# Hymba-style encoder: A's key doublings and C's gate product on VectorE, own-key products summed in PSUM, new spacing of A's levels

## The chip, the cores and the metric

The kernel runs on one core of one Trainium2 chip. Its engines are TensorE (PE; its weight loads are shown as PEld), VectorE (DVE), ScalarE (ACT), GpSimd (POOL) and SyncE (SP, which issues most transfers). The metric is the device time of one execution in microseconds: less is better.

## The reference, cut to what matters

Two layers (`DEPTH = 2`) of a mixer over 512 tokens of width 1024. In each layer the normalised input is projected by `w_in` into the inputs of four groups of 512 channels; their outputs are gated, concatenated, projected by `w_out` and added to x.

- A: a gated linear recurrence in both directions, four heads of 128 channels. Per head, with keys `k` and forget gates `f` per channel, `S_t = diag(f_t) S_{t-1} + k_t v_t^T`, `o_t = S_t^T q_t`; the sum of both directions is normalised and gated.
- B: attention within a window of 128 tokens. D: attention to 256 memory tokens.
- C: an mLSTM in both directions, four heads: values `h`, then `(h - mu) * rsqrt(var + eps) * g`, and then the product with the gate `silu(z)`.

The change touches A's recurrence and the last product of C.

## The kernel before, in words

TensorE does almost all work in fp32. A projection is three matmuls for each pair of blocks (high and low parts of weights and activations). The weights come through `load_w`: a transfer into a raw tile `wr` (three buffers), a cast on ScalarE to `wh`, and the remainder `wl = wr - wh` on VectorE, 1024 elements for each partition.

The mixers are generators ("jobs") whose steps are woven into the projections' matmuls by a planner, `Weave`. Each projection calls `tick` after every six small or three large matmuls (640 ns of planned time). A step returns `(pe, lat)`: its own TensorE time, which is added to the planner's clock, and the time after which its next step is due. A due step is emitted at the next tick; `join` emits what is left of a job at once. So `A_LAT` (4300 ns) sets how many projection matmuls stand between two levels of a head in the order in which the program is written. The framework then places each engine's instructions; within an engine they can stand in another order than they were written in, as far as their inputs allow.

`mix_A` works on one head; a pair of heads runs at a time (`group_A`, `pr` 0 and 1), the second one set off by half of `A_LAT`. The products of queries and keys are made by doubling: `K2` (keys, two directions of 512) and `Q2` (queries) hold products of gates over blocks of m tokens. At the start `ks`, the sum of both halves of K2, is made on VectorE, and `per_block` makes the products within single tokens ("own-key products") from it: 16 blocks of 32 x 32 into a PSUM bank of `psc`, which has two. Then for m = 1, 2, 4, ... 64 a level does the following:

- `per_block` with `kc`, an interleaved copy of K2 that ScalarE makes, and Q2 (from m = 32 on with K2 itself);
- the key doubling `k2v` in place, on GpSimd, by gate products `Tm`;
- the query doubling `q2v` in place, on VectorE;
- `copy_predicated` of the level's products into `ac` on VectorE (or a copy into `at`);
- the gate products of the next level, `Tn`, on VectorE (they use the tile of `ks` again as `tot`).

After the levels come transposes of K2, the states, the output products `o`, the normalisation to y, and after `A_LATN` the transposes of y. For the second pair a `join` stands between the projection `group_Dz` and C's next projections; it emits what is left of the pair.

In `stats` of group C a head is normalised on VectorE and multiplied by its gate on GpSimd; its transposes (`finish`) come one head later.

All vector instructions are recorded at line 142 and most matmuls at lines 248 (`mm`) and 251 (`gmm`), so they are told apart by tiles: `s` is a bank of `psc`, `pj` a bank of a projection, `u` and `a` are tiles of 4 KB and 2 KB for each partition (K2, Q2, F2 are `u`; `ks`, q, `ac`, the products are `a`). A key or query doubling is `u<-u,u` at level 1 and `u<-u,a` later; an own-key product is `s<-a,a`.

Of the kernel before, what the change touches and what calls it, by code (L numbers as in the profile page):

```python
# [10 lines left out]
ALU = mybir.AluOpType  # L11
# [3 lines left out]
P = 128  # L15
# [54 lines left out]
              + [O_CK, O_CQ, O_CZ, O_CZ + 256, O_DQ, O_DQ + 256])  # L70
OUT_ORDER = ((0, 1), (2, 3))

A_LAT0, A_LAT, A_LAT2, A_LATN = 5500, 4300, 500, 27000
B_LATP, B_LAT = 300, 1150
AHEAD = 2
AHEAD_V = 1
# [120 lines left out]
def trunk(tc, a, dbg=None, mark=lambda s: None):  # L197
# [6 lines left out]
    with es:  # L204
# [343 lines left out]
        def mix_A(l, hd, F2, K2, q, v, gz, yT):  # L548

            Q2 = u4([2, 512])  # L550
            ks = a2([512])
            dve.tensor_tensor(ks, K2[:, 0], K2[:, 1], ALU.add)
            dve.tensor_tensor(Q2, F2, V(q, 0, [[0, 2], [1, 512]]), ALU.mult)
            scr = u4([2, 512])
            at = scr[:, 1]
            ac = a2([NC, 32])

            kcs = (scr[:, 0], F2[:, 1])
            at4 = at.rearrange("p (c q) -> p c q", c=NC)

            def interleaved(lv, m):
                kc = kcs[lv % 2]
                act.copy(V(kc, 0, [[2 * m, 256 // m], [m, 2], [1, m]]), V(K2, 0, [[2 * m, 256 // m], [512 + m, 2], [1, m]]))
                return kc

            def per_block(n, k, qv):

                p = psc()[:, :NC * n].rearrange("p (c q) -> p c q", c=NC)
                for c in range(NC):
                    for i in range(P // n):  # L570
                        gmm(p[i * n:(i + 1) * n, c], k(c * P + i * n), qv(c * P + i * n), True, True)
                return p
            kc = interleaved(0, 1)
            yield 0, A_LAT0
            pd = per_block(32, lambda b: ks[:, b:b + 32], lambda b: q[:, b:b + 32])
            act.copy(ac, pd)
            Tm = F2
            n = 512
            tot = ks
            toff = 0  # L580
            lv = 0
            m = 1
            while m <= 64:
                k2v = V(K2, 0, [[2 * m, 256 // m], [512 + m, 2], [1, m]])
                q2v = V(Q2, 0, [[2 * m, 256 // m], [512 + m, 2], [1, m]])
                if m <= 16:
                    pl = per_block(32, lambda b: kc[:, b:b + 32],
                                   lambda b: V(Q2, b, [[2 * m, 16 // m], [512 + m, 2], [1, m]]))
                else:

                    d = lambda b: b // m % 2
                    pl = per_block(m, lambda b: K2[:, d(b), b:b + m],
                                   lambda b: Q2[:, 1 - d(b), b + m - 2 * m * d(b):b + 2 * m - 2 * m * d(b)])

                gp.tensor_tensor(k2v, k2v, V(Tm, n + 1, [[2, n // 2], [-(n + 1), 2], [0, m]]), ALU.mult)
                if 1 < m < 16:
                    kc = interleaved(lv + 1, 2 * m)
                dve.tensor_tensor(q2v, q2v, V(Tm, 1, [[2, n // 2], [n - 1, 2], [0, m]]), ALU.mult)
                if m <= 16:
                    dve.copy_predicated(ac, V(cu, lv * 32, [[0, NC], [1, 32]]), pl)  # L600
                    if m == 16:

                        act.copy(at.rearrange("p (c j q) -> p c j q", c=NC, j=4), V(ac, 0, [[32, NC], [0, 4], [1, 32]]))
                elif m == 32:
                    dve.copy_predicated(at.rearrange("p (c j q) -> p c j q", c=NC, j=4),
                                        V(cu, 5 * 32, [[0, NC], [32, 4], [1, 32]]), V(pl, 0, [[32, NC], [0, 4], [1, 32]]))
                else:
                    act.copy(at4[0:64, :, 64:128], pl[0:64])
                    act.copy(at4[64:128, :, 0:64], pl[64:128])

                if m == 1:
                    Tn = q
                else:
                    Tn = tot[:, toff:toff + n]
                    toff += n
                dve.tensor_tensor(Tn[:, 0:n].rearrange("p (d k) -> p d k", d=2),
                                  V(Tm, 0, [[n, 2], [2, n // 2]]), V(Tm, 1, [[n, 2], [2, n // 2]]), ALU.mult)
                if m == 1:
                    kc = interleaved(lv + 1, 2 * m)
                Tm = Tn  # L620
                n //= 2
                m *= 2
                lv += 1
                yield 560, A_LAT


            kb = ((0, 1, 2), (3, 2, 1))
            ktm = F2
            for d in range(2):
                pt = ptr()  # L630
                for i, j in enumerate(kb[d]):
                    nc.tensor.transpose(pt[:, i * P:(i + 1) * P], K2[:, d, j * P:(j + 1) * P], ident)
                act.copy(ktm[:, d, 0:384], pt[:, 0:384])
            yield 640, A_LAT2
            st = K2
            for d in range(2):
                pS = psc()
                for i, j in enumerate(kb[d]):
                    mm(pS[:, i * P:(i + 1) * P], ktm[:, d, i * P:(i + 1) * P], v(j))
                act.copy(st[:, d, 0:P], pS[:, 0:P])  # L640
                for i in range(1, 3):
                    dve.scalar_tensor_tensor(st[:, d, i * P:(i + 1) * P], st[:, d, (i - 1) * P:i * P],
                                             Tm[:, 4 * (1 - d) + kb[d][i]:4 * (1 - d) + kb[d][i] + 1], pS[:, i * P:(i + 1) * P],
                                             ALU.mult, ALU.add)
            yield 1280, A_LAT2
            o = po()
            for c in range(NC):
                oc = o[:, c * P:(c + 1) * P]
                mm(oc, at[:, c * P:(c + 1) * P], v(c), start=True, stop=False)
                qc = [Q2[:, i, c * P:(c + 1) * P] for i in range(2)]  # L650
                if c > 0:
                    mm(oc, qc[1], st[:, 0, (c - 1) * P:c * P], start=False, stop=(c == NC - 1))
                if c < NC - 1:
                    mm(oc, qc[0], st[:, 1, (2 - c) * P:(3 - c) * P], start=False, stop=True)
            ss = sm([4], "ssA")
            jk = scr[:, 0]
            for c in range(NC):
                act.activation(jk[:, c * P:(c + 1) * P], o[:, c * P:(c + 1) * P], AF.Square, accum_out=ss[:, c:c + 1])
            r = rsqrt(4, ss, 1.0 / P, EPS)
            y = F2[:, 0]  # L660
            for c in range(NC):
                dve.scalar_tensor_tensor(y[:, c * P:(c + 1) * P], o[:, c * P:(c + 1) * P], r[:, c:c + 1], gz(c), ALU.mult, ALU.mult)
            yield 2133, A_LATN
            pt = ptr()
            for c in range(NC):
                nc.tensor.transpose(pt[:, c * P:(c + 1) * P], y[:, c * P:(c + 1) * P], ident)
            if len(yT[0]) <= hd // 2:
                for i in range(2):
                    yT[i].append(u4([2, 512], F32R))
            y_evac(yT, hd, 0, T, pt, gA[:, l, hd:hd + 1])  # L670
            yield 427, 0

        def group_A(l, h, pr, yT, between=None, before=None, raw=None):
# [49 lines left out]
            def go():  # L723
                for b in range(2):
                    jobs.append(wv.spawn(f"mixA{pr * 2 + b}", mix_A(l, pr * 2 + b, F2[b], K2[b], q[b],
                                         lambda c, b=b: v[:, c, b * P:(b + 1) * P],
                                         lambda c, b=b: gz[:, c, b * P:(b + 1) * P], yT), after=b * A_LAT / 2))
            if pr == 0:
                gates()
                if raw is not None:  # L730
# [167 lines left out]
        def group_C(l, h):  # L898
# [195 lines left out]
            gz = []  # L1094

            def mixer(yT):
# [47 lines left out]
                def stats(hd):  # L1144

                    hc = H[hd]
                    h3 = hc.rearrange("p (c d) -> p c d", c=NC)
                    s = slice(hd % 2 * P, hd % 2 * P + P)
                    dve.scalar_tensor_tensor(h3, tho[hd // 2][:, :, s], 1.0, h3, ALU.add, ALU.mult)
                    mv = sm([4, 2], "mvC")  # L1150
                    for c in range(NC):
                        b6 = sm([6], "stC")
                        dve.bn_stats(b6, h3[:, c])
                        dve.bn_aggr(mv[:, c], b6)
                    r = rsqrt(4, mv[:, :, 1], 1.0, 4 * EPS)
                    for c in range(NC):
                        dve.tensor_scalar(h3[:, c], h3[:, c], mv[:, c, 0:1], r[:, c:c + 1], ALU.subtract, ALU.mult)
                    gp.tensor_tensor(h3, h3, gz[hd // 2][:, :, s], ALU.mult)

                def finish(hd):  # L1160
                    pt = ptr()
# [410 lines left out]
```

## Time and profile before

| | us |
|---|---|
| median of 3 runs (1136.57 to 1139.35) | 1136.97 |
| profiled execution, its own time | 1137.1 |
| its span, first to last instruction | 1135.3 |
| busy: TensorE | 1079.4 |
| busy: VectorE | 795.3 |
| busy: ScalarE | 538.3 |
| busy: GpSimd | 243.4 |

Times within the trace are from the start of the span. The records of matmuls overlap, so their busy time isn't work at full rate; what counts is where TensorE stands idle and who releases it. The mean granted clock of TensorE is 0.99.

### The profile page before, as it was taken

To read this page: it belongs to the slowest core of one execution; us is meant where nothing else is said; L and a number is where in the kernel's file an instruction comes from. 1 tells how busy PE (TensorE), PEld (TensorE's weight loads), DVE (VectorE), ACT (ScalarE), POOL (GpSimd) and SP (SyncE) were. 2 spreads that over 40 slices of the span, in tenths; PEclk is the share of its full clock that TensorE was granted. 3 is DMA by queue.
4 is the path that set the end of the run, shared out by engine and by line. 5 is a ranking of instruction groups with operands and counts; after the bars stand their busy time and mean duration, and the time that the engine had idled before them with its cause. 6 is when DMAs were issued, how large, how long until landed. Compare 5 with 4: busy or idle time off the path is not lost.

```text
span 1135.3 us, 22387 instructions
## 1 busy us (share of the span) xinstructions
PE 1079.4 (95%) x8886; PEld 968.2 (85%) x8886; DVE 795.3 (70%) x1759; ACT 538.3 (47%) x1138; POOL 243.4 (21%) x276
## 2 busy tenths in 40 slices
PE   6889999989999999999999999999899999999997
PEld 4778988989888888788788889889888788989997
DVE  7799536787486768777464786377968759688664
ACT  5545335666443534344564433376654353442443
POOL 4252000231142123111020241012304311230200
PEclk9999999999999999999999999999999999999998
DMA  7222134111221444422434221311121233362211
GB/s 255 77 94 76 57 104 158 59 57 45 88 75 58 108 107 122 148 76 92 134 128 142 81 67 58 98 62 56 58 75 57 76 108 98 103 195 77 74 38 74
DMA packets 34783, 105.41 MB, mean 93 GB/s; under 512 B 4360, under 2 KB 7816, under 8 KB 34680
## 3 DMA queue, kind: packets, MB, share of 16 engines
q1 hardware_dynamic: 33960, 101.57, 28.4%
q0 software_dynamic: 720, 2.42, 0.6%
q8 instruction: 70, 1.15, 0.4%
q14 instruction: 33, 0.27, 0.1%
HBM read 99.72 MB, written 4.26 MB: 92 GB/s over the span
## 4 chain that ended last, share of the span: by engine, by line
PE 71%; DVE 18%; ACT 3%; issue 2%; DMA 1%; POOL 0%; SPq 0%; DVEq 0%; ACTq 0%; POOLq 0%
PE pj L248 33%; PE pj L251 23%; DVE a L142 7%; DVE u L142 5%; PE o L248 4%; DVE wl L142 3%; PE s L248 3%; PE s L251 2%; ACT wh L142 1%; PE tr L857 1%; PE o L251 1%; ACT u L142 1%; ACT a L142 1%; DVE rq_t L142 1%; PE tr L1290 1%
## 5 line engine op out<-in xcount | busy, mean ns | idle before, releaser
L251 PE MATMUL pj<-wh,u 128*128 128x256 f32 x1984 | 390.7, 287 | 3.2 <-ACT u L142 1.2
L248 PE MATMUL pj<-u,wh 128*128 128x512 f32 (+1 forms) x1216 | 376.8, 391 | 1.0 <-ACT a L142 0.8
L251 PEld LDWEIGHTS pj<-wh,u 128*128 128x128 f32 x1984 | 317.0, 190 | 8.2 <-ACT u L142 2.4
L142 DVE TENSOR_TENSOR wl<-wr,wh 128x1024 fp32r<-128x1024 f32 (+1 forms) x162 | 215.4, 1330 | 135.8 <-ACT wh L142 135.3
L251 PE MATMUL pj<-wl,u 128*128 128x256 f32 x992 | 280.7, 283 | 0.0
L248 PEld LDWEIGHTS pj<-u,wh 128*128 128x128 f32 x1216 | 219.2, 190 | 42.5 <-ACT a L142 1.2
L248 PE MATMUL pj<-u,wl 128*128 128x512 f32 (+1 forms) x608 | 234.0, 385 | 1.8 <-DVE wl L142 1.8
L142 ACT CAST wh<-wr 128x1024 fp32r<-128x1024 f32 (+1 forms) x162 | 164.1, 1014 | 151.1 <-PE pj L248 88.0
L251 PEld LDWEIGHTS pj<-wl,u 128*128 128x128 f32 x992 | 188.3, 190 | 0.8 <-issue 0.3
L248 PEld LDWEIGHTS pj<-u,wl 128*128 128x128 f32 x608 | 115.4, 190 | 25.3 <-DVE wl L142 2.0
L142 POOL TENSOR_TENSOR u<-u,a 128x512 f32<-128x512 f32 (+1 forms) x64 | 93.2, 1464 | 133.0 <-PE s L251 53.5
L142 POOL TENSOR_SCALAR u<-u,rB 128x256 f32<-128x256 f32 (+1 forms) x64 | 37.3, 595 | 232.9 <-DVE rB L142 132.5
L142 POOL TENSOR_TENSOR u<-u,u 128x512 f32<-128x512 f32 x16 | 29.3, 1830 | 210.9 <-DVE a L142 125.0
L248 PE MATMUL pj<-wh,u 128*128 128x256 f32 (+1 forms) x320 | 62.8, 287 | 0.0
L142 DVE TENSOR_TENSOR u<-u,a 128x512 f32<-128x512 f32 (+1 forms) x56 | 50.2, 897 | 15.9 <-PE s L251 13.5
L248 PE MATMUL o<-u,u 128*128 128x129 f32 (+1 forms) x384 | 50.2, 275 | 1.9 <-DVE dnC L142 1.9
L248 PEld LDWEIGHTS o<-u,u 128*128 128x128 f32 x384 | 48.2, 191 | 4.4 <-issue 2.4
L248 PEld LDWEIGHTS pj<-wh,u 128*128 128x128 f32 x320 | 51.0, 188 | 0.7 <-issue 0.5
L251 PEld LDWEIGHTS s<-u,u 128*32 128x32 f32 (+1 forms) x1760 | 27.4, 115 | 28.1 <-issue 19.3
L251 PE MATMUL s<-u,u 128*32 128x32 f32 (+2 forms) x1760 | 35.0, 207 | 17.2 <-DVE a L142 13.6
L142 ACT COPY u<-u 128x512 f32<-128x512 f32 x40 | 27.0, 684 | 40.7 <-DVE u L142 22.8
L248 PE MATMUL pj<-wl,u 128*128 128x256 f32 (+1 forms) x160 | 45.3, 283 | 0.0
(213 smaller groups left out, 1494.3 us busy)
## 6 DMA issues: line engine op xcount, KB each, us to landing
wr<-in_wpk SPq DMA_DIRECT2D x154, 512.0 KB, 3.3
u<-in_xT SPq DMA_DIRECT2D x16, 256.0 KB, 4.6
u<-rdr SPq DMA_DIRECT2D x16, 256.0 KB, 4.5
u<-gdr SPq DMA_DIRECT2D x16, 192.0 KB, 5.8
u<-in_memT SPq DMA_DIRECT2D x4, 512.0 KB
xd<-u POOLq DMA_DIRECT2D x4, 512.0 KB, 4.8
u<-xd SPq DMA_DIRECT2D x4, 512.0 KB, 5.4
out<-u SPq DMA_DIRECT2D x8, 256.0 KB, 2.0
```

The costliest lines, as they stand in the source:

```text
L142: r = f(*args, **kw)
L248: nc.tensor.matmul(out, l, r, start=start, stop=stop)
L251: nc.tensor.matmul(out, l, r, start=start, stop=stop, skip_group_check=True)
L857: nc.tensor.transpose(pt[:, j * P:(j + 1) * P], pr[e][:, j * P:(j + 1) * P], ident)
L1290: nc.tensor.transpose(pt[:, (2 * t + i) * P:(2 * t + i + 1) * P], pr[:, i, t * P:(t + 1) * P], ident)
```

## The change

The key doubling of all seven levels is made by VectorE instead of GpSimd, and so is C's product with the gate. The sum `ks` is gone; `per_block` takes several keys and sums their products in PSUM, so that the own-key products are two matmuls for each block, with the two halves of K2. `tot` gets a tile of its own, allocated after them. `A_LAT` becomes 5400 for the first pair and 4600 for the second, and the offset of a pair's second head becomes half of that.

```diff
--- before.py
+++ after.py
@@ -70,7 +70,7 @@
               + [O_CK, O_CQ, O_CZ, O_CZ + 256, O_DQ, O_DQ + 256])
 OUT_ORDER = ((0, 1), (2, 3))
 
-A_LAT0, A_LAT, A_LAT2, A_LATN = 5500, 4300, 500, 27000
+A_LAT0, A_LAT, A_LAT2, A_LATN = 5500, (5400, 4600), 500, 27000
 B_LATP, B_LAT = 300, 1150
 AHEAD = 2
 AHEAD_V = 1
@@ -548,8 +548,6 @@
         def mix_A(l, hd, F2, K2, q, v, gz, yT):
 
             Q2 = u4([2, 512])
-            ks = a2([512])
-            dve.tensor_tensor(ks, K2[:, 0], K2[:, 1], ALU.add)
             dve.tensor_tensor(Q2, F2, V(q, 0, [[0, 2], [1, 512]]), ALU.mult)
             scr = u4([2, 512])
             at = scr[:, 1]
@@ -563,20 +561,23 @@
                 act.copy(V(kc, 0, [[2 * m, 256 // m], [m, 2], [1, m]]), V(K2, 0, [[2 * m, 256 // m], [512 + m, 2], [1, m]]))
                 return kc
 
-            def per_block(n, k, qv):
+            def per_block(n, qv, *ks):
+
 
                 p = psc()[:, :NC * n].rearrange("p (c q) -> p c q", c=NC)
                 for c in range(NC):
                     for i in range(P // n):
-                        gmm(p[i * n:(i + 1) * n, c], k(c * P + i * n), qv(c * P + i * n), True, True)
+                        for k in ks:
+                            gmm(p[i * n:(i + 1) * n, c], k(c * P + i * n), qv(c * P + i * n), k is ks[0], k is ks[-1])
                 return p
             kc = interleaved(0, 1)
             yield 0, A_LAT0
-            pd = per_block(32, lambda b: ks[:, b:b + 32], lambda b: q[:, b:b + 32])
+
+            pd = per_block(32, lambda b: q[:, b:b + 32], lambda b: K2[:, 0, b:b + 32], lambda b: K2[:, 1, b:b + 32])
             act.copy(ac, pd)
             Tm = F2
             n = 512
-            tot = ks
+            tot = a2([512])
             toff = 0
             lv = 0
             m = 1
@@ -584,15 +585,15 @@
                 k2v = V(K2, 0, [[2 * m, 256 // m], [512 + m, 2], [1, m]])
                 q2v = V(Q2, 0, [[2 * m, 256 // m], [512 + m, 2], [1, m]])
                 if m <= 16:
-                    pl = per_block(32, lambda b: kc[:, b:b + 32],
-                                   lambda b: V(Q2, b, [[2 * m, 16 // m], [512 + m, 2], [1, m]]))
+                    pl = per_block(32, lambda b: V(Q2, b, [[2 * m, 16 // m], [512 + m, 2], [1, m]]),
+                                   lambda b: kc[:, b:b + 32])
                 else:
 
                     d = lambda b: b // m % 2
-                    pl = per_block(m, lambda b: K2[:, d(b), b:b + m],
-                                   lambda b: Q2[:, 1 - d(b), b + m - 2 * m * d(b):b + 2 * m - 2 * m * d(b)])
-
-                gp.tensor_tensor(k2v, k2v, V(Tm, n + 1, [[2, n // 2], [-(n + 1), 2], [0, m]]), ALU.mult)
+                    pl = per_block(m, lambda b: Q2[:, 1 - d(b), b + m - 2 * m * d(b):b + 2 * m - 2 * m * d(b)],
+                                   lambda b: K2[:, d(b), b:b + m])
+
+                dve.tensor_tensor(k2v, k2v, V(Tm, n + 1, [[2, n // 2], [-(n + 1), 2], [0, m]]), ALU.mult)
                 if 1 < m < 16:
                     kc = interleaved(lv + 1, 2 * m)
                 dve.tensor_tensor(q2v, q2v, V(Tm, 1, [[2, n // 2], [n - 1, 2], [0, m]]), ALU.mult)
@@ -621,7 +622,7 @@
                 n //= 2
                 m *= 2
                 lv += 1
-                yield 560, A_LAT
+                yield 560, A_LAT[hd // 2]
 
 
             kb = ((0, 1, 2), (3, 2, 1))
@@ -724,7 +725,7 @@
                 for b in range(2):
                     jobs.append(wv.spawn(f"mixA{pr * 2 + b}", mix_A(l, pr * 2 + b, F2[b], K2[b], q[b],
                                          lambda c, b=b: v[:, c, b * P:(b + 1) * P],
-                                         lambda c, b=b: gz[:, c, b * P:(b + 1) * P], yT), after=b * A_LAT / 2))
+                                         lambda c, b=b: gz[:, c, b * P:(b + 1) * P], yT), after=b * A_LAT[pr] / 2))
             if pr == 0:
                 gates()
                 if raw is not None:
@@ -1155,7 +1156,7 @@
                     r = rsqrt(4, mv[:, :, 1], 1.0, 4 * EPS)
                     for c in range(NC):
                         dve.tensor_scalar(h3[:, c], h3[:, c], mv[:, c, 0:1], r[:, c:c + 1], ALU.subtract, ALU.mult)
-                    gp.tensor_tensor(h3, h3, gz[hd // 2][:, :, s], ALU.mult)
+                    dve.tensor_tensor(h3, h3, gz[hd // 2][:, :, s], ALU.mult)
 
                 def finish(hd):
                     pt = ptr()
```

## Rows read from the trace of the kernel before

**Rows 1.** The page's part 1: busy us, share of the span, instructions.
```profile
PE 1079.4 (95%) x8886; PEld 968.2 (85%) x8886; DVE 795.3 (70%) x1759; ACT 538.3 (47%) x1138; POOL 243.4 (21%) x276
```

**Rows 2.** Busy time by stretch, A's first five levels, instructions in brackets, granted clock.
```profile
60.00:92.00 32.00, 25.36 (x482) 23.30 (x482) 31.14 (x45) 12.93 (x20) 15.34 (x10) 1.00 0.30 98
300.00:332.00 32.00, 29.90 (x480) 27.45 (x479) 27.48 (x36) 14.81 (x23) 17.81 (x10) 1.00 0.21 67
636.00:664.00 28.00, 24.28 (x419) 22.67 (x418) 27.11 (x35) 12.87 (x20) 16.24 (x10) 1.00 0.18 59
856.00:886.00 30.00, 27.40 (x462) 25.80 (x461) 29.18 (x36) 13.50 (x21) 16.91 (x10) 0.94 0.17 58
```
The columns: stretch and its length, then PE, PEld, DVE, ACT, POOL, PE clock, DMA share, GB/s.

**Rows 3.** TensorE's timeline, last pair: start, length, idle before in square brackets, releaser.
```profile
866.50 0.46 PE L251 MATMUL s<-a,a 128*32 128x32 f32 x32
868.76 0.54 PE L251 MATMUL s<-u,u 128*32 128x32 f32 x32 [1.79 <-DVE a L142]
```

**Rows 4.** VectorE's timeline in the same pair.
```profile
863.95 2.91 DVE L142 TENSOR_TENSOR wl<-wr,wh 128x1024 fp32r<-128x1024 f32 x1 [0.34 <-ACT wh L142]
...
868.32 0.29 DVE L142 COPY_PREDICATED a<-cu,s 128x128 f32<-128x128 uint8 x1
...
877.34 0.69 DVE L142 TENSOR_TENSOR u<-u,a 128x512 f32<-128x512 f32 x1
...
883.95 2.12 DVE L142 TENSOR_TENSOR wl<-wr,wh 128x1024 fp32r<-128x1024 f32 x1
```

**Rows 5.** GpSimd's timeline in the same pair.
```profile
863.79 2.00 POOL L142 TENSOR_TENSOR u<-u,u 128x512 f32<-128x512 f32 x1 [3.83 <-DVE a L142]
...
883.35 1.63 POOL L142 TENSOR_TENSOR u<-u,a 128x512 f32<-128x512 f32 x1 [0.68 <-ACT u L142]
```

**Rows 6.** VectorE's groups, 856 to 886: count, busy us, mean ns of one.
```profile
L142 DVE TENSOR_TENSOR wl<-wr,wh 128x1024 fp32r<-128x1024 f32 x4 | 10.0, 2503 | 0.7 <-ACT wh L142 0.7
L142 DVE TENSOR_TENSOR u<-u,a 128x512 f32<-128x512 f32 x4 | 4.4, 1100 | 0.0
L142 DVE TENSOR_TENSOR a<-u 128x512 f32<-128x512 f32 x4 | 4.1, 1018 | 0.0
...
L142 DVE TENSOR_TENSOR u<-u,u 128x512 f32<-128x512 f32 x2 | 2.2, 1090 | 0.0
```

**Rows 7.** All weight splits: nanoseconds, shortest, median, longest.
```profile
L142 DVE TENSOR_TENSOR wl<-wr,wh x162: 410/1225/2985, 7.1 to 1111.4; 128x1024 fp32r<-128x1024 f32 x154, 128x256 fp32r<-128x256 f32 x8
```

**Rows 8.** The chain that ended last, first pair, levels and end: start, length, what.
```profile
95.36 0.39 PE s L251 x32
95.74 3.02 PE pj L251 x24
...
118.43 0.22 PE o L248 x2
118.65 0.71 PE pj L251 x6
119.36 2.05 PE o L248 x18
```

**Rows 9.** TensorE's timeline, first pair, own-key products and level 1.
```profile
63.23 0.46 PE L251 MATMUL s<-a,a 128*32 128x32 f32 x32
63.50 0.56 PE L251 MATMUL s<-u,u 128*32 128x32 f32 x32
```

**Rows 10.** The chain that ended last, end of the last pair.
```profile
916.97 2.01 PE o L248 x18
918.98 5.35 PE pj L248 x23
924.33 0.87 PE tr L666 x8
```

**Rows 11.** VectorE's timeline, end of the last pair and `stats` in C.
```profile
923.06 1.12 DVE L142 SCALAR_TENSOR_TENSOR u<-o,rq_y,u 128x128 f32<-128x128 f32 x4
...
1009.97 1.11 DVE L142 TENSOR_SCALAR u<-u,mvC,rq_y 128x128 f32<-128x128 f32 x4
1011.00 0.16 DVE L142 RECIPROCAL dnC<-dnC 128x2 f32<-128x2 f32 x1
```

## The prediction

> **What bounds the kernel now.** I read the page's engine totals first [rows 1]: TensorE's records cover 95% of the span, VectorE's 70%. The kernel is bound by TensorE, so an edit is worth what it gives TensorE back: idle time before a matmul, added matmuls, or time at the low clock. The totals don't say where that idle lies, so next I cut out the four stretches in which group A runs its first five levels (two heads at once, two pairs, two layers) [rows 2]. TensorE is idle there for 6.64, 2.10, 3.72 and 2.60 us, 15.1 us together. VectorE is nearly full in three of them (31.14 of 32, 27.11 of 28, 29.18 of 30 us). The last stretch also has a mean granted clock of 0.94: in 30 us that is 1.8 us of full-speed clock lost.
>
> What does TensorE wait for? In the last stretch it stands 1.79 us before the level-1 products of the second head, and the releaser is a VectorE write of an `a` tile [rows 3]. The small products have two PSUM banks (`psc`), so the second head's products need the bank that the first head's `copy_predicated` still has to read. That instruction stands on VectorE at 868.32, behind a weight split `wl` that began at 863.95 and took 2.91 us [rows 4].
>
> Why does that split take 2.91 us? The median of all splits is 1.225 us [rows 7]. GpSimd began a key doubling at 863.79, which ended at 865.79 [rows 5]; from there to the split's end (866.86) are 1.07 us, about a split's own length. So the split seems to have stood until GpSimd was done. Another such pair is the split at 883.95 (2.12) beside the doubling at 883.35 (1.63) [rows 4, 5]. A key doubling on GpSimd is paid on VectorE as a stretched instruction.
>
> How much is paid? The grouped rows of that stretch [rows 6] against the unstretched durations: four splits 4 x (2.503 - 1.225) = 5.1 us; four query doublings 4 x (1.100 - 0.69) = 1.6; four `a<-u` of the same size 4 x (1.018 - 0.69) = 1.3, 0.69 being the clean row at 877.34 [rows 4]. With nothing counted for smaller instructions that is 8.1 us for the ten doublings of the stretch, 0.81 us each.
>
> **The change part by part.** *Doublings to VectorE.* Fifty-six move (8 heads x 7 levels). On VectorE a doubling is the twin of the query doubling: same shape, same pattern. That twin takes 0.69 us clean [rows 4], and 1.09 at level 1 (`u<-u,u`), where the pattern hops between halves at every element [rows 6]. A stretch has two of the long and eight of the short: 2 x 1.09 + 8 x 0.69 = 7.7 us added, 8.1 us of stretching removed. I keep both ends: if none of the stretching goes, VectorE gains 7.7 us of work; if all goes, it is relieved by 0.4. I take the second, for the start and end times above.
>
> *The sum `ks` goes.* Two of the four `a<-u` of a stretch, 2 x 0.69 = 1.4 us off VectorE. In all that relieves it by 1.8 us in a stretch where TensorE stands idle for 2 to 7 us; the rest has to come from the spacing.
>
> *A new wait.* The own-key products now read K2 itself, and level 1 doubles K2 in place; so the first doubling may start only when these products are done. Before, it ran ahead: the second head's at 863.79 [rows 5], its own-key products at 866.50 [rows 3]. Behind them VectorE now has a burst for each head: doubling 1.09, query doubling 1.09, `copy_predicated` 0.29, 2.5 us before the bank is free. TensorE reaches the second head's products after two planner ticks (12 matmuls, 1.5 us, half of the row of 24 [rows 8]) and 0.5 us of own-key products, so 0.5 us late in the second pairs, up to 1.7 if a split gets in between. In the first pairs the second head starts 2700 behind instead of 2150, a third tick, 0.8 us more: 0 to 0.9 late. I take about the middle, 2 x 1.0 + 2 x 0.4 = 2.8 us for four stretches. Behind the doubling on its engine stand the splits, and TensorE's projections wait for these; three raw buffers cover that.
>
> (`tot` takes a buffer of its own from a pool of 16; the first product that needs it runs after a whole level, and I count nothing.)
>
> *Later levels.* A period of two heads is now two groups of small products and 36 projection matmuls, 2 x 0.39 + 1.5 x 3.02 = 5.3 us of TensorE work [rows 8]. VectorE needs two query doublings (1.4), two `copy_predicated` (0.6), a split (1.2) and the stretching of two doublings (1.6): 4.8, and whatever else is in line. After: 4 x 0.69 + 0.6 + 1.2 = 4.6.
>
> *Spacing.* A head's next level is emitted at the first tick of 640 ns past its due time, with the other head's 560 ns counted in: 4300 needs 6 ticks, 4600 needs 7, 5400 needs 8. A tick is six matmuls, 0.8 us. So the period becomes 6.9 us in first pairs and 6.1 in second ones, against 4.6 of need. I count nothing left after level 1: idle goes from 15.1 to 2.8, **-12.3 us**. The projections fill the wider gaps; no work is added.
>
> *Clock.* The low clock of the last stretch follows the 1.79 us wait. Similar waits in the other stretches were not followed by one [rows 2], so I take half of 1.8: **-0.9**.
>
> *Own-key products twice.* 32 records in 0.46 us, the next group's start 0.27 after its own [rows 9]. The change doubles them for 8 heads: 8 x 0.27 = **+2.2 us**, on the engine that bounds. From below, 0 where TensorE would wait anyway; from above 8 x 0.46 = 3.7. This row gives 8.4 ns from one of these matmuls to the next. The Trainium skill, page "TensorE: Matmul & The Clock Gate", section "Wait — 56ns, not 53.3ns?", says that the start-to-start of matmuls never falls below about 25 ns however few the columns. By that floor the 256 added records would be 6.4 us (an estimate from the page); the trace disagrees for these 32-column tiles.
>
> *C's gate product.* Eight products of 512 elements, about 0.69 us each on VectorE. TensorE's path is there at one place for each layer: the reciprocal that the value products wait for stands right behind the four scalings that the product follows (1009.97, 1011.00 [rows 11]), so 2 x 0.6 = **+1.2** (0 if it is placed behind, 8 x 0.69 = 5.5 if all show).
>
> *The end of second pairs.* Seven levels x one tick put the last A products 7 x 0.8 = 5.6 us of projection work later, while the transposes stay behind Dz's last matmul. Now 5.35 us lie between them [rows 10], and the last write of y ends at 924.18 [rows 11], as the transposes begin. In fixed order TensorE would then wait. But its order isn't fixed: one A step is split by projection matmuls (o x2 at 118.43, o x18 at 119.36 [rows 8]), so unready work is passed over. I take 0.3 for each layer, **+0.6**, of a possible 2 x 5.
>
> **Sum.** 1137.1 - 12.3 - 0.9 + 2.2 + 1.2 + 0.6 = 1127.9. The profiled execution stands 0.1 above the median of the runs, so **1128 us**. What lies outside the span (1.8 us) stays.
>
> **The rivals.** (a) *Half stays.* VectorE serves its line in order; a doubling placed ahead of what TensorE wants gives back half of the wait: 1137.1 - 7.5 + 2.2 + 1.2 = 1133. For it: the new wait at level 1. Against: the wide spacing. (b) *The wait moves to the y transposes,* 4.5 us or so for each layer, 1128 + 9 = 1137. For it: the two times in [rows 10, 11]. Against: the split step. (c) *Slower: VectorE becomes the bound.* If the stretched records are not stretched by GpSimd, ten doublings less two `ks` put 7.7 - 1.4 = 6.3 us into each stretch; four times that, less the 7.1 us that VectorE is idle in them [rows 2], is 18.1: 1137.1 + 18.1 + 3.4 = 1158.6. VectorE's load grows once less than 0.63 of the 0.81 us per doubling goes away, and past that the wider spacing has to cover it. Against: in the pairs named above the excess is as long as GpSimd's overlap. (d) *All idle goes:* 1137.1 - 15.1 - 1.8 + 2.2 = 1122.4. (e) *The added products run slower when two add into one block:* at three times the 8.4 ns, +4.3, 1132. For it: no row shows two different weights adding there. The floor that the Trainium skill's page "TensorE: Matmul & The Clock Gate" gives, named above, would come out about there.
>
> **Chances.** Forecast (1124 to 1132) 0.60; (a) 0.13; (b) 0.09; (c) 0.06; (d) 0.09; (e) 0.03. A measurement tells about 0.3% from no change: faster is under 1133.6, slower over 1140.4. Faster: 0.60 + 0.09 + 0.03 and two thirds of (a), 0.81. Same: the rest of (a) and (b), less a little for a worse order elsewhere, 0.12. Slower: (c) and that, 0.07. The range 1121 to 1135.5 leaves (b) and (c) out.
>
> **What would show it.** Right: in the four stretches no split over 1.5 us, TensorE idle under 1.5 us in each, key doublings at 0.69 on VectorE, groups of 64 own-key records. Wrong: long splits without GpSimd at work (c), a wait before the y transposes (b), a wait before the second head's level 1 of 2 us or more (a). A different order of VectorE's work in B or C, which this trace can't show, would shift the time by a few us either way.

## The result and the profile after

The changed kernel took 1122.63 us (median of 4 runs, 1122.14 to 1126.58) beside 1136.93 of the kernel before: a ratio of 0.9877, 95% interval 0.9851 to 0.9903, 14.3 us less. In a second comparison it had 1123.96 us and 0.9871 (0.9844 to 0.9898). The forecast was 1128.0; the time is nearer to that of rival (d), 1122.4. The profiled execution is the one of 1126.58 (span 1124.7); the other three were within 1122.14 to 1122.73.

The page's part 1 after, which answers to [rows 1]:

```profile
PE 1083.0 (96%) x9142; PEld 972.2 (86%) x9142; DVE 780.0 (69%) x1815; ACT 538.7 (48%) x1138; POOL 140.8 (13%) x212
```

VectorE has 56 instructions more and is busy 15.3 us less. GpSimd gave away 64 instructions and 102.6 us.

Busy time by stretch for A's first five levels, each cut from the first own-key product to the end of level 5, in the columns of [rows 2]:

```profile
62.90:97.80 34.90, 33.96 (x670) 31.82 (x669) 33.76 (x86) 17.13 (x27) 0.00 (x0) 1.00 0.32 99
304.90:334.50 29.60, 29.60 (x611) 26.13 (x611) 23.73 (x49) 11.97 (x20) 0.00 (x0) 1.00 0.24 74
636.50:669.90 33.40, 33.40 (x671) 31.62 (x671) 26.96 (x56) 12.87 (x22) 0.00 (x0) 1.00 0.25 81
854.80:884.30 29.50, 29.50 (x610) 26.16 (x610) 23.69 (x49) 12.05 (x20) 0.00 (x0) 1.00 0.24 74
```

TensorE is idle for 0.94 us in the first stretch and not at all in the others: 0.94 in place of 15.1. VectorE is still nearly full in the first (1.1 us free) and has 5.8 to 6.4 us free in the others; GpSimd does nothing there.

VectorE's timeline in the last pair, for [rows 4, 6]:

```profile
855.78 2.13 DVE L142 TENSOR_TENSOR u<-u,u 128x512 f32<-128x512 f32 x2
857.76 0.30 DVE L142 COPY_PREDICATED a<-cu,s 128x128 f32<-128x128 uint8 x1
...
861.33 0.67 DVE L142 TENSOR_TENSOR u<-u,a 128x512 f32<-128x512 f32 x1
...
864.57 1.21 DVE L142 TENSOR_TENSOR wl<-wr,wh 128x1024 fp32r<-128x1024 f32 x1
...
870.21 1.22 DVE L142 TENSOR_TENSOR wl<-wr,wh 128x1024 fp32r<-128x1024 f32 x1
```

The first row is the pair of level 1: key doubling and query doubling, 2.13 us together. From level 2 on a doubling takes 0.67. The splits in the four stretches take 1.21 to 1.24 us each; before, the mean of those in the last one was 2.503 [rows 6].

The chain of waits at the end of the last pair, for [rows 10]:

```profile
908.91 2.01 PE o L248 x18
910.92 0.47 PE pj L248 x2
911.39 0.44 PE tr L667 x4
911.82 5.60 PE pj L248 x24
...
917.50 0.30 PE tr L667
917.80 0.23 PE pj L248
```

The y transposes, eight in one piece before, are now split by projection matmuls. Nothing waits here.

Last, two stretches of 30 us with their granted clock, the third number from the end:

```profile
450.00:480.00 30.00, 29.64 (x151) 25.34 (x152) 23.39 (x79) 10.81 (x17) 0.00 (x0) 0.94 0.29 98
...
990.00:1020.00 30.00, 28.14 (x203) 26.58 (x203) 25.54 (x81) 10.85 (x22) 5.84 (x5) 0.94 0.54 172
```

A mean of 0.94 over 30 us is 1.8 us lost. The low clock of the last pair [rows 2] is gone (1.00 in 854.8 to 884.3), but others stand in this execution, in other work. Cut into stretches of 30 us, it has seven at 0.93 to 0.95 ahead of its end, the kernel before has five. Its mean clock is 0.987; the three faster runs have 0.991 to 0.993.

### The profile page after: what moved, and what is told of

It is laid out like the page before. It is cut to its first block, busy times and chain, and to the rows that moved or that the text cites. A ratio compares the mean times of both kernels' runs of the same rounds, so it can differ in the third digit from the quotient of the medians.

```text
span 1124.7 us, 22824 instructions
## 1 busy us (share of the span) xinstructions
PE 1083.0 (96%) x9142; PEld 972.2 (86%) x9142; DVE 780.0 (69%) x1815; ACT 538.7 (48%) x1138; POOL 140.8 (13%) x212
## 4 chain that ended last, share of the span: by engine, by line
PE 77%; DVE 13%; ACT 3%; issue 2%; DMA 1%; POOL 0%; SPq 0%; DVEq 0%; ACTq 0%; POOLq 0%
PE pj L248 32%; PE pj L251 29%; DVE a L142 5%; PE o L248 4%; PE s L248 3%; PE s L251 3%; DVE u L142 3%; DVE wl L142 3%; PE tr L858 1%; PE o L251 1%; ACT a L142 1%; ACT wh L142 1%; ACT u L142 1%; DVE rq_t L142 1%; PE tr L1291 1%
## 5 line engine op out<-in xcount | busy, mean ns | idle before, releaser
L142 DVE TENSOR_TENSOR wl<-wr,wh 128x1024 fp32r<-128x1024 f32 (+1 forms) x162 | 197.0, 1217 | 132.0 <-ACT wh L142 130.9
L142 DVE TENSOR_TENSOR u<-u,a 128x512 f32<-128x512 f32 (+1 forms) x104 | 74.1, 730 | 19.7 <-PE s L251 15.9
L142 POOL TENSOR_TENSOR u<-u,cf 128x512 f32<-128x512 f32 x16 | 24.2, 1510 | 234.1 <-DMA u<-rdr 234.1
L142 DVE TENSOR_TENSOR u<-u,u 128x512 f32<-128x512 f32 (+2 forms) x48 | 38.8, 841 | 3.8 <-ACT a L142 2.6
L248 PE MATMUL s<-u,a 128*128 128x256 f32 (+1 forms) x224 | 41.3, 303 | 0.0
L142 DVE TENSOR_TENSOR u<-pj,u 128x256 f32<-128x256 f32 (+2 forms) x52 | 24.9, 502 | 21.4 <-PE pj L248 14.6
```

Source lines behind the costliest of these rows:

```text
L142: r = f(*args, **kw)
L248: nc.tensor.matmul(out, l, r, start=start, stop=stop)
```

## Experiments

All times are medians; ratios are to the kernel before on the same chip, with 95% intervals. "Alone" is the kernel before with one part, "undone" the changed kernel without one part.

### Each part alone

**The doublings alone.**

```
-                gp.tensor_tensor(k2v, k2v, V(Tm, n + 1, ...), ALU.mult)
+                dve.tensor_tensor(k2v, k2v, V(Tm, n + 1, ...), ALU.mult)
```

> The kernel before with one part alone: the 56 key doublings of A on VectorE instead of GpSimd; the key sum, the spacing of 4300 and C's gate product stay as before. Theory (a key doubling on GpSimd is paid on VectorE as a stretched instruction of up to its own length): in A's four stretches no weight split over 1.5 us, VectorE's busy time over the span not higher than before but lower by some 10 us, TensorE's idle time in the four stretches from 15.1 to under 6 us, and a time of about 1137 - 10 = 1127 us, so most of the gain of the whole change. Rival 1 (spacing does it): the burst of doublings stays ahead of the waits, idle in the stretches stays above 10 us, 1134 to 1138 us. Rival 2 (the long instructions are not GpSimd's doing): 10 x 0.77 us more on VectorE in each stretch, 1150 us or more.

Measured: 1118.6 us, ratio 0.9838 (0.9820 to 0.9855). The page's part 1, and the first and the last of the four stretches, cut in the same way:

```profile
PE 1077.7 (96%) x8886; PEld 967.9 (87%) x8886; DVE 778.3 (70%) x1815; ACT 539.5 (48%) x1138; POOL 150.7 (13%) x220
```

```profile
62.90:91.50 28.60, 28.50 (x569) 26.57 (x567) 28.29 (x62) 13.38 (x22) 0.00 (x0) 1.00 0.35 112
...
849.90:876.60 26.70, 26.55 (x538) 23.68 (x537) 22.16 (x47) 11.39 (x20) 0.00 (x0) 1.00 0.23 71
```

One word of the diff gives more than the whole change, and the theory held with more than it expected (1127 us, VectorE relieved by some 10 us). TensorE's idle time in all four is 0.48 us (0.10, 0.09, 0.14, 0.15), at the old spacing. VectorE took over 56 doublings (48 of 0.68 and 8 of 1.07, 41 us) and is busy 17.0 us less: so 58 us of stretching went, 1.04 us for each doubling.

**The spacing alone.**

```
-A_LAT0, A_LAT, A_LAT2, A_LATN = 5500, 4300, 500, 27000
+A_LAT0, A_LAT, A_LAT2, A_LATN = 5500, (5400, 4600), 500, 27000
```

> The kernel before with one part alone: A's spacing 5400 for the first pair and 4600 for the second instead of 4300; the doublings stay on GpSimd, the key sum and C's gate product stay. Theory (stretching is the cost, spacing only leaves room): long splits of 1.5 to 2.9 us stay, VectorE's busy time stays within 3 us of before, and the wider spacing hides some of the waits: idle in the four stretches from 15.1 to 6 to 11 us, 1129 to 1134 us. Rival 1 (spacing does it): idle under 3 us, 1124 to 1127 us.

Measured: 1135.2 us, 0.9990 (0.9978 to 1.0002). Both expectations missed. Two of its stretches, the first and the last pair, and the splits of the last:

```profile
60.00:92.00 32.00, 27.43 (x463) 25.66 (x462) 30.86 (x48) 14.56 (x21) 16.02 (x10) 0.95 0.30 97
...
854.00:886.00 32.00, 29.08 (x484) 27.12 (x482) 30.43 (x38) 14.00 (x22) 16.68 (x10) 1.00 0.22 79
```

```profile
L142 DVE TENSOR_TENSOR wl<-wr,wh 128x1024 fp32r<-128x1024 f32 x4 | 9.4, 2352 | 0.6 <-ACT wh L142 0.6
```

Idle is 4.57 us in the first stretch (6.64 before) and 2.92 in the last (2.60 in 30 us before), and a split still takes 2.35 us on average. VectorE is busy 7.3 us less (788.0), so a part of the stretching did go, but the rest still stands in TensorE's way: cut from the own-key products to the end of level 5, the four stretches have 12.4 us of idle time in place of 15.1. Of these 2.7 us the clock takes back some 1.7: two of the four stretches lose that much to a low clock here, one before. What is left, 1.0 us, is what the medians differ by.

**The own-key products alone.**

```
-            ks = a2([512])
-            dve.tensor_tensor(ks, K2[:, 0], K2[:, 1], ALU.add)
...
-            pd = per_block(32, lambda b: ks[:, b:b + 32], lambda b: q[:, b:b + 32])
+            pd = per_block(32, lambda b: q[:, b:b + 32], lambda b: K2[:, 0, b:b + 32], lambda b: K2[:, 1, b:b + 32])
```

> The kernel before with one part alone: the key sum gone and the own-key products accumulated from both key halves (256 matmul records more), doublings on GpSimd, spacing 4300, C's gate product on GpSimd. Theory: TensorE +1.7 to +2.2 us; VectorE loses 8 sums of 0.69 us; the level-1 doubling on GpSimd may start only after the own-key products and no longer runs ahead, so the stretching and the wait fall into the second head's level 1. About 1137, from 1134 to 1141 us. Rival (TensorE has a floor of some 25 ns from one matmul to the next): +6.4 us of TensorE work, 1140 to 1144 us.

(`tot` gets a tile of its own with it.) Measured: 1144.8 us, 1.0078 (1.0059 to 1.0097): slower by 8.6 us, past the theory's range and just past the rival's. But the rival's reason doesn't hold; the price per matmul record is below ("the own-key products undone"). What grew is the waiting: in the profiled execution, 11.7 us longer than that of before, TensorE is idle for 22.9 us in the four stretches in place of 15.1. VectorE's and GpSimd's timelines at level 1 of the last pair show where it comes from:

```profile
875.29 2.96 DVE L142 TENSOR_TENSOR u<-u,u 128x512 f32<-128x512 f32 x1
878.11 0.28 DVE L142 COPY_PREDICATED a<-cu,s 128x128 f32<-128x128 uint8 x1
...
879.14 2.55 DVE L142 TENSOR_TENSOR u<-u,u 128x512 f32<-128x512 f32 x1 [0.18 <-PE s L251]
```

```profile
874.76 2.53 POOL L142 TENSOR_TENSOR u<-u,u 128x512 f32<-128x512 f32 x1 [34.01 <-PE s L251]
879.12 1.55 POOL L142 TENSOR_TENSOR u<-u,a 128x512 f32<-128x512 f32 x1 [1.83 <-ACT u L142]
880.63 2.81 POOL L142 TENSOR_TENSOR u<-u,u 128x512 f32<-128x512 f32 x1
```

The level-1 doubling on GpSimd no longer runs ahead: it is released by TensorE's own-key products, at 874.76, and now lies beside the query doubling, which ends 0.96 us after it (2.96 us long in place of 1.09 [rows 6]). Behind that stands the `copy_predicated` that frees TensorE's bank. The second head's query doubling (879.14) stands in the same way behind the key doubling at 879.12, which ends at 880.67. So this part is bad beside GpSimd's doublings and less bad without them.

**C's gate product alone.**

```
-                    gp.tensor_tensor(h3, h3, gz[hd // 2][:, :, s], ALU.mult)
+                    dve.tensor_tensor(h3, h3, gz[hd // 2][:, :, s], ALU.mult)
```

> The kernel before with one part alone: C's gate product (8 of 512 elements) on VectorE instead of GpSimd. Theory by the prediction: +0.6 us for each layer in front of the reciprocal that the value products wait for, +1.2 us, 1138.2 us. Rival: it takes away the stretching that the product on GpSimd causes on VectorE in C, as in A, and the time is the same or 1 to 2 us less, 1135 to 1137 us.

Measured: 1138.05 us, 1.0014 (1.0003 to 1.0026), 1.6 us more; the prediction's +1.2 lies within the interval. The chain of waits in layer 1 of this kernel, and the wait of TensorE at its end, in the kernel before and in this one:

```profile
1011.77 0.07 DVE dnC L142
1011.84 0.92 DVE u L142 x2
```

```profile
1012.09 1.13 PE L248 MATMUL o<-u,u 128*128 128x129 f32 x8 [0.71 <-DVE dnC L142]
```

```profile
1012.91 1.43 PE L248 MATMUL o<-u,u 128*128 128x129 f32 x8 [0.86 <-DVE dnC L142]
```

The product is in the chain, but one place later than forecast: behind the reciprocal (`dnC` at 1011.77), in the 0.92 us with the first division. It adds only 0.15 us to the wait: before, the division there stood 0.44 us for ScalarE. The rest isn't in that wait. In this execution the granted clock falls right behind it (0.94 in 1000 to 1030, 1.00 before), which loses 1.8 us; whether the product brings that about isn't shown.

### One part undone, and the whole again

**The own-key products undone:** the key sum is back; all else as in the changed kernel.

> The changed kernel with one part undone: VectorE adds the two key halves again and the own-key products read the sum (256 matmul records fewer); doublings and C's gate product on VectorE and the wide spacing stay. The doublings alone gave 1118.6 us, 4 us less than the whole change. Theory (the accumulated own-key products cost these 4 us: 1.7 to 2.2 us of matmuls and, for the rest, the level-1 doubling that has to wait for them): 1118 to 1120 us. Rival (C's gate product and the spacing cost them): 1121.5 us or more.

Measured: 1118.55 us, 0.9835 (0.9811 to 0.9858), beside 0.9871 of the whole. The intervals of this pair overlap; but of the kernels made of this change's parts with the doublings on VectorE, the three with the key sum took 1118.5 to 1118.6 us, the three with accumulated products 1121.4 to 1124.0. The chain of waits in the first pair of this kernel, and then of the changed one:

```profile
57.92 3.78 PE pj L251 x32
61.71 0.76 PE s L251 x64
62.47 2.32 PE pj L251 x18
64.78 0.76 PE s L251 x64
```

```profile
63.07 1.13 PE s L251 x82
64.20 2.34 PE pj L251 x18
66.54 1.13 PE s L251 x86
67.67 3.73 PE pj L251 x30
71.40 0.31 PE s L251 x21
71.71 0.93 issue
72.64 0.32 PE s L251 x11
```

Own-key products and level 1 together grow from 0.76 to 1.13 us (some records are missing in the counts of the second): 0.37 us for 32 more matmul records, 11.6 ns each, 8 x 0.37 = 3.0 us. The 0.93 at 71.71 comes on top, in the middle of the first head's level 2. For it the profile names no releaser; it is 0.65 at the same place with C's product undone, 1.38 in the midst of a projection at 72.53 with the spacing undone, and isn't there where the key sum is kept. Its cause stays open. 3.0 + 0.9 = 3.9 is about what the medians give (4.1 and 5.4 against the two medians of the changed kernel).

**The spacing undone:** 4300 for both pairs.

> The changed kernel with one part undone: spacing 4300 for both pairs; doublings and C's gate product on VectorE and the accumulated own-key products stay. Spacing alone took 1 us from the kernel before. Theory (with VectorE relieved of the stretching, 5.3 us for two heads is room enough for the later levels, but the first head's doubling burst at level 1 now comes after its own-key products): 1 to 4 us slower than the changed kernel, 1123.5 to 1126.5 us, with the idle time in front of the second head's level-1 products. Rival (the spacing does nothing any more): 1122 to 1123 us.

Measured: 1123.09 us, 0.9872 (0.9851 to 0.9894). The rival is right: the spacing gives nothing that these runs can tell. The wait that the theory expected isn't there either: TensorE doesn't stand before the second head's level 1 in any of the four stretches.

**C's product undone:** back on GpSimd.

> The changed kernel with one part undone: C's gate product back on GpSimd. Alone it made the kernel before 1.6 to 1.8 us slower. Theory (it stands on VectorE in front of the reciprocal that the value products wait for, whatever A does): 1120.5 to 1121.5 us. Rival (a placement effect of that one kernel): 1122 to 1123 us.

Measured: 1121.37 us, 0.9860 (0.9839 to 0.9880). Lower by 1.3 to 2.6 us than the two medians of the whole, in the theory's range, but within the interval of the whole. Where the key sum was kept, the product on VectorE cost nothing (1118.55 above, 1118.52 below). Its price is somewhere between 0 and 2.6 us; these runs leave it open.

**The whole, again.**

> The changed kernel itself, timed beside the three above on the same chip: 1122 to 1123 us.

Measured: 1123.96 us (1119.34 to 1126.67), 0.9871. Its six runs have mean granted clocks of 0.987 to 0.996, and by and large follow them: 1126.67 us at 0.987, 1122.39 at 0.992, 1119.34 at 0.994.

### Is it GpSimd that stretches VectorE?

In the doublings-alone kernel, one line is added behind the key doubling; nobody reads what it writes.

```
+                gp.tensor_tensor(V(spare, ...), V(Tm, n + 1, ...), V(Tm, n + 1, ...), ALU.mult)
```

> Doublings alone on VectorE (1118.6 us), and added to it 56 products on GpSimd, one behind each key doubling, that multiply the level's gate tile with itself in the doubling's pattern and write a spare tile of bf16 that nobody reads. VectorE gets no work and no new wait. Theory (a VectorE instruction beside a GpSimd instruction with two SBUF inputs stands until that one is done): VectorE's busy time grows by about 0.8 x 56 = 45 us or at least 25 us, splits over 1.5 us are back in A's stretches, and the time goes up by 10 to 25 us, to 1128 to 1143 us. Rival (the long instructions were due to the doublings' own data, to the waits or to the order): busy time within 3 us, 1118 to 1120 us.

```
+                gp.tensor_scalar(V(spare, ...), V(Tm, n + 1, ...), 1.0, 1.0, ALU.mult, ALU.mult)
```

> As the kernel with 56 spare products on GpSimd, but each takes one input (the level's gate tile times 1.0) in place of two. Theory (what stands in VectorE's way is the second input: in the kernel before, GpSimd's one-input instructions lay beside few long VectorE records): VectorE's busy time up by less than 8 us, 1118 to 1122 us. Rival (any GpSimd instruction stretches VectorE by its length): 56 x about 0.6 = 34 us more on VectorE, 1125 us or more.

Measured: 1149.32 us, 1.0121 (1.0099 to 1.0143) with two inputs, 30.7 us over the kernel without the line; 1127.69 us, 0.9922 (0.9907 to 0.9937) with one, 9.1 us over. VectorE's busy time goes from 778.3 to 818.5 and 796.3. A GpSimd and a VectorE row of the first, then of the second kernel:

```profile
73.53 1.15 POOL L143 TENSOR_TENSOR spare<-a 128x512 bf16<-128x512 f32 x1 [0.29 <-DVE a L143]
73.71 1.52 DVE L143 TENSOR_TENSOR u<-u,a 128x512 f32<-128x512 f32 x1
```

```profile
74.01 0.72 POOL L143 TENSOR_SCALAR spare<-a 128x512 bf16<-128x512 f32 x1 [0.29 <-DVE a L143]
74.17 1.09 DVE L143 TENSOR_TENSOR u<-u,a 128x512 f32<-128x512 f32 x1
```

The doubling (0.68 alone) ends 0.55 us after GpSimd's end in the first (75.23 against 74.68) and 0.53 in the second: it stands until GpSimd is done, whichever instruction that is. The theory of the two-input line held (40 us, 1149 us is even past its 1143), but for one sign: the splits in the levels stay at 1.2 to 1.5 us, and what is stretched is the doublings and other products. TensorE's idle time in the four stretches, 0.48 us without the line, is 25.0. The theory for a single input failed (18.0 us of stretching, not under 8). A one-input instruction costs less because it is shorter, not because it leaves VectorE alone: in these rows GpSimd's is 0.43 us shorter (0.72 against 1.15), and so is the doubling beside it (1.09 against 1.52).

The Trainium skill, page "SBUF — State Buffer", section "Who interferes with whom", says that a VectorE instruction with two SBUF inputs contends with a GpSimd instruction that reads SBUF, and that the ports which the two engines share are an exclusive lock. These pairs agree, for GpSimd instructions with one input too.

### Two versions

**Doublings and spacing, nothing else.**

> Doublings on VectorE and the wide spacing, with the key sum kept and C's gate product on GpSimd: the two parts of the change that did not cost anything by themselves. Theory (parts add): 1117 to 1119 us, the least of all so far. Rival (the spacing is worth nothing once VectorE is relieved): as the doublings alone, 1118.6, within 0.5.

Measured: 1118.52 us, 0.9840 (0.9825 to 0.9855): the rival, 0.1 us from the doublings alone.

**Doublings, and C's mask additions on VectorE.**

```
-                        gp.tensor_tensor(own, own, V(mge if d == 0 else mle, ...), ALU.add)
+                        dve.tensor_tensor(own, own, V(mge if d == 0 else mle, ...), ALU.add)
```

> Doublings alone on VectorE (1118.6 us), and in C the 16 mask additions of 512 elements on VectorE too (GpSimd spends 1.437 us on each). Theory (the same exchange as in A: what VectorE takes on it gets back in stretching): VectorE's busy time within 4 us, 1116.5 to 1119.5 us. Rival (C has little for VectorE to wait behind, so the additions only delay what TensorE waits for, as the gate product did): 1120 to 1123 us.

Measured: 1115.42 us (1113.73 to 1117.22), 0.9812 (0.9797 to 0.9828): better than both kernels, and below both expected ranges. Sixteen additions of 0.69 us came to VectorE, 11.0 us, and its busy time grew by 1.5 (778.3 to 779.8): the same exchange as in A. Against the doublings alone it is 3.2 us less, though the two intervals overlap a little and its mean clock is a little higher (0.990 to 0.995 beside 0.990 to 0.993).

## Why the prediction was right, and where its size was off

**What bounds the kernel, and the stretching: right.** TensorE's idle time in A went, and it went because the doublings left GpSimd: the doublings alone bring 18.4 us (0.9838 of 1136.97; 17.6 between the medians of their own comparison), and putting GpSimd work beside them takes all of it back. Rival (c), that the long records were not GpSimd's doing, is out. The signs that were named for being right all stand in the changed kernel: splits of 1.24 us at most in the four stretches, at most 0.94 us of idle time in each, key doublings of 0.67 to 0.7 (1.1 at level 1), own-key products in groups of 64 records.

**The price of the stretching: too small.** The prediction took 0.81 us for each doubling, "with nothing counted for smaller instructions"; measured are 1.04. Hence the wrong reading that follows from it, that moving the doublings relieves VectorE by little and "the rest has to come from the spacing". The spacing brings nothing in any of three comparisons. What moved in the forecast's sum by spacing, the doublings did. In effect rival (d) came true, that all idle goes, which the prediction gave a chance of 0.09.

**The new wait at level 1: didn't come.** This term put the forecast too high by 2.8 us. The first doubling does wait for the own-key products, but TensorE doesn't wait for it. The chain of waits of the changed kernel in the last pair:

```profile
854.89 1.13 PE s L251 x83
856.01 1.61 PE pj L251 x12
857.63 1.13 PE s L251 x86
```

The prediction's burst on VectorE is there, 2.3 us in place of 2.5: doubling, query doubling and `copy_predicated` run from 855.78 to 858.06, and begin behind the own-key products (854.89 to about 855.5). For TensorE the prediction counted 12 projection matmuls and the second head's own-key products, 2.0 us. It left out the first head's level-1 products, which stand in between (the 1.13 of the first group holds both), and the own-key products are longer. So TensorE comes to the second head's level 1 at 858.22 by its timeline, 2.7 us after the end of the first own-key products, and the bank has been free since 858.06: VectorE is 0.2 us early in place of 0.5 late.

**The rest of the sum.** Idle kept, 0.94 in place of 2.8; the clock of the last stretch, 1.8 gained in place of 0.9; the end of second pairs, 0 in place of 0.6; own-key products 0.8 dearer: 1127.9 - 1.9 - 0.9 - 0.6 + 0.8 = 1125.3. The two medians lie 1.3 and 2.7 us below that. The profiled execution (1126.6, mean clock 0.987) lies above it, the other three (1122.1 to 1122.7, 0.991 to 0.993) below: what is left is of the size of the clock's falls, and C's product (1.2 in this sum, perhaps less) is in it too. Between the two profiled executions the account closes by the pages' part 1: over the whole span TensorE is idle 14.2 us less (1135.3 - 1079.4 = 55.9 before, 1124.7 - 1083.0 = 41.7 after), 14.1 of it in the four stretches, and busy 3.6 us more, of which the own-key products are 3.0. So the forecast was right to look for the idle time in those stretches alone.

**Own-key products twice: right, a little small.** 3.0 us against 2.2; 11.6 ns for each added record in place of the 8.4 of [rows 9]. A row that the prediction had at hand was nearer: a group of 32 records takes 0.39 us in the chain of [rows 8], which makes 8 x 0.39 = 3.1. Rival (e), three times 8.4 ns, is out. The Trainium skill, page "TensorE: Matmul & The Clock Gate", section "Wait — 56ns, not 53.3ns?", gives a floor of about 25 ns from one matmul to the next, by which the same records would have cost 6.4 us (an estimate from the page). These matmuls with 32 columns stay under it.

**C's product:** +1.2 forecast, 0 to 2.6 measured. The place was one instruction off, behind the reciprocal and ahead of the division, and the wait there grew by 0.15 us in place of 0.6.

**The y transposes (rival b):** no wait; the step is split, as the prediction read from [rows 8].

**The whole** is thus one edit that gives 18.4 us and one that takes 4 to 5 back, with two that do little. In the forecast's sum the second one is there (2.2 + 2.8 = 5.0), but as two terms of a change that needed all its parts; that it could be left out, and the time be 1118.6, wasn't seen. It is luck that these 5.0 us are near the 4 to 5 measured: 2.8 of them stand for a wait that didn't come, by 0.2 us, and 0.9 of the measured cost is one that nobody forecast.

## What to carry to other kernels

Price a GpSimd instruction at what it costs VectorE too: here a key doubling takes 1.1 to 2.9 us on GpSimd, stretches VectorE by 1.04 on average, and takes 0.7 on VectorE itself (1.1 at level 1), so the "relief" costs more than the work. Before an instruction is left on GpSimd for want of time on VectorE, compare VectorE's record lengths beside GpSimd's with the clean ones; where they are longer, moving the work relieves both. And when a change has several parts, time each alone: a part that replaces an addition by matmuls on the engine that bounds was paid by the others.

## What the runs showed of the hardware

Tiny VectorE instructions are held as well. In C, where [rows 11] lie, the changed kernel's VectorE and GpSimd (four elements for each partition; clean such rows take 0.16):

```profile
991.26 0.16 DVE L142 TENSOR_TENSOR rq_t<-rq_y 128x4 f32<-128x4 f32 x1
991.46 1.16 DVE L142 SCALAR_TENSOR_TENSOR rq_t<-rq_t,rq_v 128x4 f32<-128x4 f32 x1
992.65 0.94 DVE L142 SCALAR_TENSOR_TENSOR rq_y<-rq_t,rq_y 128x4 f32<-128x4 f32 x1
```

```profile
991.33 1.27 POOL L142 TENSOR_TENSOR u<-u,cf 128x512 f32<-128x512 f32 x1 [1.00 <-DMA u<-rdr]
992.56 1.01 POOL L142 TENSOR_TENSOR u<-u,a 128x384 f32<-128x384 f32 x1
```

The two end at 992.62 and 993.59, within 0.03 us of GpSimd's ends (992.60 and 993.57): six to seven times their length. And the effect runs through to the time almost undamped: 40.2 us of stretching on an engine that is busy for 70% of the span made the kernel 30.7 us longer, because it fell into the stretches where VectorE stands in front of TensorE's banks (25.0 us of idle time there, 0.48 without it).
